# Gate and decay masks of a gated delta rule: GpSimd products replaced by ScalarE row scalings and one more accumulating matmul

## The chip, the core and the metric

The kernel runs on one core of a Trainium2 chip. The core has a matrix engine (TensorE, PE in the profile; PEld are its weight loads), a vector engine (VectorE, DVE), an activation engine (ScalarE, ACT), a general engine (GpSimd, POOL), and a queue that issues the transfers (SyncE, SP). Each engine works through its own list of instructions in order; between engines, an instruction waits until a semaphore says that its inputs are there. Matmuls write to PSUM banks of 128 x 512 float32 values; everything else lies in SBUF, as tiles of 128 partitions.

The metric is the time of one launch in device microseconds. A profile is one such launch, recorded by the hardware.

## What is computed

One decoder layer for 1024 prompt tokens (with zero state) and 8 x 8 sample tokens (each of the 8 sequences with a state of its own). One input projection feeds three groups: a convolution module, eight heads of a gated delta rule, and cross-attention into 256 memory tokens. Their outputs, gated, go through one output projection, and a layer norm follows. Cut to the delta rule, which the change touches:

```python
gcum = jnp.cumsum(g, axis=-1)                      # log decay, per head and token
incl = pos[:, None] >= pos[None, :]
decay = jnp.exp(jnp.where(incl, gcum[..., :, None] - gcum[..., None, :], -jnp.inf))
kb = k * beta[..., None]
m = jnp.where(strict, jnp.einsum("bnhik,bnhjk->bnhij", kb, k) * decay, 0.0)
tinv = lax.linalg.triangular_solve(eye + m, ...)
a_qk = jnp.einsum("bnhik,bnhjk->bnhij", q, k) * decay
def step(s, xs):                                   # chunk after chunk
    u = u0_c - jnp.einsum("bhck,bhkv->bhcv", w_c, s)
    o = jnp.einsum("bhck,bhkv->bhcv", qd_c, s) + jnp.einsum("bhij,bhjv->bhiv", aqk_c, u)
    s = s * gl_c + jnp.einsum("bhck,bhcv->bhkv", kd_c, u)
    return s, o
```

So each chunk needs a square matrix `decay`, the exponential of the difference of two running sums of `g`, zero where the second token comes later than the first. All inputs and outputs are float32.

## The kernel before

**Passes.** The input projection runs twice over its weights: first over the first 512 prompt tokens with the 64 sample tokens (576 columns, in two banks of 288), then over the last 512 prompt tokens (one bank of 512). A pass has 52 column tiles of 128 outputs, ordered by `ct_order`: for each head k, q, v and its gate, then the convolution's columns, then those of the memory. The first pass has the memory's own projection before column tile 44. Then comes the output projection in two groups of token tiles.

**Precision.** Float32 inputs are split in two parts of type fp32r, a high one (ACT copies it: `wh`, `xh`) and a low one (the rest, `wl`, `xl`, made by DVE, or by POOL for every other quarter up to the 450th). A product takes three fp32r matmuls (`mm3`). Weights arrive as 128 x 1024 pieces (`raw`) and are split in quarters of 512 columns (`split_quarter`). `gemm` calls `ensure(2)` ahead of a quarter's matmuls, so that two further quarters have been issued to ACT, DVE and POOL by then. There are four buffers for `wh` and four for `wl`.

**Side work.** Everything else (convolutions, delta rule, attention) is written as Python generators in a list, `Side`. After every group of matmuls `tick` steps those that are ready. Whether one is ready is asked of a planner, `Model`, that keeps a clock for each engine and a cost for each kind of instruction: for ACT 100 + 0.83 ns per element and 93 ns for each scale or bias that is a tile, for POOL's product of two tensors 100 + 2 ns per element, for an fp32r matmul its columns by 2.4 GHz. So the order of instructions on every engine is fixed when the program is built, and costs in the planner decide it. The four PSUM banks for side work are handed out by `getps` and given back by `relps`, at the planner's later clock of ACT and DVE.

**The delta rule.** A unit is one head in one pass: 512 tokens as four chunks of 128, so 16 units in all. `gen_gates` gives, for each pass, `gh` and `gl`, the high and low part of g. For a unit `gen_k` does, in this order: the products `gmh` and `gml` of the upper triangle `triu` (ones where column is at or past row) with g, for four chunks (lines 590 and 591); transposes of k and their squares (`jk`); two matmuls with `trilr`, the strict lower triangle, which add up g between two tokens for all four chunks in one bank `psD` (608, 609); `D`, its exponential, by ACT (611); the norms of k and beta (`kz`, `kzn`, 614 to 617); a power for v's scale (618); four products k by k in `psKK`; then `Dm` = D times `triu` (626), which clears what lies below the diagonal, and `D` times `kzn`, minus beta over the squared norm of k (628), both on POOL; `Y`, the product of `psKK` and D, on DVE (631). Y goes through DRAM into a solve by rows on DVE (`xt`, `X`, 652 to 656) and small matmuls (`U`). `gen_q` multiplies q by k with `Dm` (723), `gen_v` scales v, and `gen_chain` steps through the four chunks.

`gen_s` does the same for the sample tokens of a head, once per head in the first pass. Two tiles `S0` hold the eight states. After the matmul that reads them (896) and the solve's result `ut` (909) POOL multiplies them by their decay `egs` (911); `ux` repeats `ut` four times, masked by `bm4` (918), and ACT squares the output (`sqs`, 920).

`bc` repeats a matrix along a middle axis without a copy, `bl` repeats a column of values along the last axis.

Of the kernel before, what the change touches and what calls it, by code (L numbers as in the profile page):

```python
# [8 lines left out]
F32 = mybir.dt.float32  # L9
F32R = mybir.dt.float32r  # L10
AF = mybir.ActivationFunctionType
ALU = mybir.AluOpType
# [4 lines left out]
P = 128  # L17
# [144 lines left out]
def hybrid_step(ctx, tc, I, O):  # L162
    nc = tc.nc
    md = Model()
    act, dve, pool, pe, sp = (
        Proxy(md, n, e)
        for n, e in (("ACT", nc.scalar), ("DVE", nc.vector), ("POOL", nc.gpsimd), ("PE", nc.tensor), ("SP", nc.sync))
    )
# [8 lines left out]
    cst = sctx.enter_context(tc.tile_pool(name="cst", bufs=1))  # L177
# [6 lines left out]
    def nm(s):  # L184
        uid[0] += 1
        return f"{s}{uid[0]}"

    def W(shape, dt=F32, name="w"):
        return wk.tile(shape, dt, tag="W", bufs=NW, name=nm(name))

    def T5(shape, dt=F32, name="t"):
        return wk.tile(shape, dt, tag="T5", bufs=N5, name=nm(name))

    def Z(shape, name="z"):
        return wk.tile(shape, F32, tag="Z", bufs=NZ, name=nm(name))
# [4 lines left out]
    def getps(name="ps"):  # L200
        while live[0] >= 4 or min(freed) > md.clk["PE"]:
            yield "B"
        freed.remove(min(freed))
        live[0] += 1
        return pss.tile([P, 512], F32, tag="s", name=nm(name))
# [9 lines left out]
    def relps(n=1):  # L215
        live[0] -= n
        freed.extend([max(md.clk["ACT"], md.clk["DVE"]) + 100] * n)
# [79 lines left out]
    Y = {}  # L297
# [50 lines left out]
    ident = cst.tile([P, P], F32, name="ident")  # L348
    ones = cst.tile([P, P], F32, name="ones")
    triu = cst.tile([P, P], F32, name="triu")  # L350
    tril = cst.tile([P, P], F32, name="tril")
    trilr = cst.tile([P, P], F32R, name="trilr")
    bl8r = cst.tile([P, P], F32R, name="bl8r")
    bu8 = cst.tile([P, P], F32, name="bu8")
    auq = cst.tile([P, P], F32, name="auq")
    LV = (1, 2, 4)
# [3 lines left out]
    bm4 = cst.tile([P, 4], F32, name="bm4")  # L360
# [12 lines left out]
    def sel(out, in_, base, pattern, cm, fill=0.0):  # L373
        pool.affine_select(out=out, in_=in_, compare_op=ALU.is_ge, fill=fill, base=base, pattern=pattern,
                           channel_multiplier=cm)
# [2 lines left out]
    sel(tril, ones, -1, [[-1, P]], 1)  # L378
    sel(ident, triu, 0, [[-1, P]], 1)
    pool.tensor_copy(out=trilr, in_=tril)  # L380


    def bat(x):
# [51 lines left out]
    def bc(m, n=4):  # L435
        return m.unsqueeze(1).to_broadcast([m.shape[0], n, m.shape[1]])

    def bl(z, n, w):
        return z.unsqueeze(2).to_broadcast([z.shape[0], n, w])
# [86 lines left out]
    def transposes(ps, src, n=4, rows=P, cols=P):  # L526
        for c in range(n):
            pe.transpose(out=ps[0:cols, c * rows:(c + 1) * rows], in_=src[:, c * cols:(c + 1) * cols],
                         identity=ident[0:rows, 0:rows])

    def g3(ps, n=4, w=P):
        return ps[:, 0:n * w].rearrange("p (c n) -> p c n", c=n)

# [48 lines left out]
    def gen_k(u):  # L582
        p, h = u["p"], u["h"]
        while gates[p] is None or "ok_k" not in u:
            yield "B"
        gt = gates[p]
        u["gt"] = gt
        gmh = W([P, 4, P], F32R, name="gmh")
        gml = W([P, 4, P], F32R, name="gml")
        pool.tensor_tensor(out=gmh, in0=bc(triu), in1=bl(gt["gh"][:, 0:4, h].bitcast(F32), 4, P), op=ALU.mult)  # L590
        pool.tensor_tensor(out=gml, in0=bc(triu), in1=bl(gt["gl"][:, 0:4, h], 4, P), op=ALU.mult)
        kT = u["kT"]
        yield (kT,)
        psK = yield from getps()
# [3 lines left out]
        zn = Z([P, 4], name="kzn")  # L598
        kd = W([P, 4, P], name="kd")
        for c in range(4):  # L600
            jk = T5([P, P], name="jk")
            act.activation(out=jk, in_=psK[:, c * P:(c + 1) * P], func=AF.Square, accum_out=ss[:, c:c + 1])
        dve.tensor_tensor(out=kd, in0=g3(psK), in1=bl(gt["ed"][:, 0:4, h], 4, P), op=ALU.mult)
        relps()
        u["kd"] = kd
        yield (gmh, gml)
        psD = yield from getps()
        pe.matmul(out=psD, lhsT=trilr, rhs=gmh.rearrange("p a b -> p (a b)"), start=True, stop=False)
        pe.matmul(out=psD, lhsT=trilr, rhs=gml.rearrange("p a b -> p (a b)"), start=False, stop=True)
        D = W([P, 4, P], name="D")  # L610
        act.activation(out=D, in_=g3(psD), func=AF.Exp)
        relps()
        yield (z,)
# [7 lines left out]
        psKK = yield from getps()  # L621
        for c in range(4):
            pe.matmul(out=psKK[:, c * P:(c + 1) * P], lhsT=kT[:, c * P:(c + 1) * P], rhs=kT[:, c * P:(c + 1) * P],
                      start=True, stop=True)
        Dm = W([P, 4, P], name="Dm")
        pool.tensor_tensor(out=Dm, in0=D, in1=bc(triu), op=ALU.mult)
        u["Dm"] = Dm
        pool.tensor_tensor(out=D, in0=D, in1=bl(zn, 4, P), op=ALU.mult)
        yield (D,)
        Y = W([P, 4, P], name="Y")  # L630
        dve.tensor_tensor(out=Y, in0=g3(psKK), in1=D, op=ALU.mult)
        relps()
        n = nunit[0]
        nunit[0] += 1
# [41 lines left out]
        for c in range(4):  # L676
            for q in range(2):
                e, o = 64 * q, 64 * q + 32
                pe.matmul(out=ps[o:o + 32, 32 * c:32 * c + 32], lhsT=Y[e:e + 32, c, o:o + 32], rhs=Rc[e:e + 32, c],
                          start=True, stop=True)  # L680
# [6 lines left out]
        for c in range(4):  # L687
            for q in range(2):
                e, o = 64 * q, 64 * q + 32
                pe.matmul(out=ps[e:e + 32, 32 * c:32 * c + 32], lhsT=Pc[o:o + 32, c], rhs=Uc[o:o + 32, c], start=True,  # L690
                          stop=True)
# [13 lines left out]
        for c in range(4):  # L705
            pe.matmul(out=ps[0:64, 256 + 64 * c:320 + 64 * c], lhsT=P6[64:128, c], rhs=U[64:128, c, 64:128],
                      start=True, stop=True)
# [117 lines left out]
    def gen_s(u):  # L825
        h = u["h"]
        while not ("ok_k" in u and "ok_q" in u and "ok_v" in u) or gates[0] is None:
            yield "B"
        gt = gates[0]
        kq, vx = u["kq"], u["vx"]  # L830
        S0 = []
        for i in range(2):
# [3 lines left out]
        gmh, gml = (T5([P, P], F32R, name=n) for n in ("gmsh", "gmsl"))  # L836
        pool.tensor_scalar(out=gmh, in0=bu8, scalar1=gt["gh"][:, 4, h:h + 1].bitcast(F32), scalar2=0.0, op0=ALU.mult,
                           op1=ALU.add)
# [24 lines left out]
        D = T5([P, P], name="Ds")  # L863
        act.activation(out=D, in_=ps[:, 0:128], func=AF.Exp)
        Y, A = T5([P, P], name="Ys"), T5([P, P], name="As")
# [29 lines left out]
        for g in range(4):  # L895
            pe.matmul(out=ps[32 * g:32 * g + 32, 0:256], lhsT=kq[:, 32 * g:32 * g + 32],
                      rhs=S0[g // 2][:, 2 * (g % 2):2 * (g % 2) + 2, :].rearrange("p b v -> p (b v)"), start=True,
                      stop=True)
        r = T5([P, P], name="rs")
        dve.scalar_tensor_tensor(out=r, in0=ps[:, 0:128], scalar=gt["cs"][:, 0, h:h + 1], in1=vs, op0=ALU.mult,  # L900
                                 op1=ALU.add)
        dve.scalar_tensor_tensor(out=r, in0=ps[:, 128:256], scalar=gt["cs"][:, 1, h:h + 1], in1=r, op0=ALU.mult,
                                 op1=ALU.add)
# [4 lines left out]
        ut = T5([P, P], name="uts")  # L908
        dve.tensor_scalar(out=ut, in0=ps[:, 0:128], scalar1=B, scalar2=None, op0=ALU.mult)
        for i in range(2):  # L910
            pool.tensor_tensor(out=S0[i], in0=S0[i], in1=bl(gt["egs"][:, h, 4 * i:4 * i + 4], 4, P), op=ALU.mult)
        yield (ut,)
        pe.matmul(out=ps[:, 128:256], lhsT=A, rhs=ut, start=True, stop=True)
        o = T5([P, P], name="os")
        dve.tensor_tensor(out=o, in0=r, in1=ps[:, 128:256], op=ALU.add)
        relps()
        ux = W([P, 4, P], name="ux")
        pool.tensor_tensor(out=ux, in0=bc(ut), in1=bl(bm4, 4, P), op=ALU.mult)
        sq2 = T5([P, P], name="sqs")
        act.activation(out=sq2, in_=o, func=AF.Square, accum_out=z[:, 5:6])  # L920
        dve.scalar_tensor_tensor(out=z[:, 5:6], in0=z[:, 5:6], scalar=1.0 / P, in1=cq, op0=ALU.mult, op1=ALU.add)
# [4 lines left out]
        for v in range(0, 4, 2):  # L926
            for i in range(2):
                rows = slice(64 * i, 64 * i + 64)
                pe.matmul(out=psl[i][:, 128 * v:128 * v + 256], lhsT=kd[rows],
                          rhs=ux[rows, v:v + 2, :].rearrange("p a b -> p (a b)"), start=True, stop=True)  # L930
# [244 lines left out]
    def finish(p, t, psl):  # L1175
# [9 lines left out]
        if COL_Q <= c < COL_DGATE:  # L1185
# [13 lines left out]
            xr, xs = evac_qkv(p, ci, psl)  # L1199
            side.add(gen_conv4(p, ci, xr, xs, u, key))  # L1200
            side.add({"k": gen_k, "q": gen_q, "v": gen_v}[key](u))
            if key == "v":
                if p == 0:
                    side.add(gen_s(u))
                side.add(gen_chain(u))
# [468 lines left out]
```

## Time and profile before

| | us |
|---|---|
| median of three runs | 2069.68 |
| the three runs | 2062.01, 2069.68, 2070.32 |
| the profiled execution | 2062.28 |
| its span, first to last instruction | 2060.6 |

The mean clock that TensorE was granted is 0.990 of full speed.

The busy time of the engines in 40 equal slices of the span, each digit a tenth (9 is 90% or more), shows the stages: the first pass up to about slice 18, the second to about slice 31, then the output projection.

```profile
PE   8999999999999989999999999999989999999995
DVE  7777877887789984255787776779985433348447
ACT  5444444444433345364444444443326522235124
POOL 6434333343323242113333333322322100006003
```

A row of the grouped view names line, engine, operation, the tile written and the tiles read, the shapes, and the count; then the busy time of the group and the mean of one in ns; then how long the engine stood idle just before these instructions and what ended that. A row of the timeline has the start, the length (of several merged instructions together), and in brackets the idle time before. A row of the waits says who waited for whom: total, times, longest. Most instructions carry line 86, the planner's wrapper through which they are issued, so they are told apart by their tiles.

### The profile page before, as it was taken

How to read it: one execution, taken by the hardware profiler on the slowest of the kernel's cores; microseconds unless marked ns; L12 is line 12 of the kernel's file. 1: busy time of each engine (PE TensorE's matmuls, PEld its weight loads, DVE VectorE, ACT ScalarE, POOL GpSimd, SP SyncE). 2: the span in 40 equal slices, each digit the busy share in tenths (PEclk: the TensorE clock that was granted, in tenths of full speed). 3: DMA queues.
4: the chain of work that ended last, by engine and by line, in shares of the span. 5: the costliest groups of instructions: out<-in, count | busy, mean ns of one | idle time of the engine just before them, and what ended most of it. 6: DMA issues, size and time to landing. Idle time of an engine off the chain costs nothing. (4 is left out here: it accounts for less than half of the span.)

```text
span 2060.6 us, 33195 instructions
## 1 busy us (share of the span) xinstructions
PE 1973.7 (96%) x12156; PEld 1708.8 (83%) x12156; DVE 1429.6 (69%) x3190; ACT 844.7 (41%) x2013; POOL 605.7 (29%) x680
## 2 busy tenths in 40 slices
PE   8999999999999989999999999999989999999995
PEld 7999999999999969977777887787767788877784
DVE  7777877887789984255787776779985433348447
ACT  5444444444433345364444444443326522235124
POOL 6434333343323242113333333322322100006003
PEclk9999999999999999999999999999999999999998
DMA  5333233323233355354332223332232563345444
GB/s 205 93 100 93 88 96 102 102 82 99 86 99 97 104 165 167 109 176 149 96 93 89 76 89 104 102 93 82 90 102 92 156 205 105 106 159 182 141 132 144
DMA packets 107267, 239.50 MB, mean 116 GB/s; under 512 B 32224, under 2 KB 36576, under 8 KB 106848
## 3 DMA queue, kind: packets, MB, share of 16 engines
q1 hardware_dynamic: 107104, 237.39, 36.5%
q8 instruction: 95, 1.56, 0.3%
q14 instruction: 68, 0.56, 0.1%
HBM read 210.24 MB, written 27.10 MB: 115 GB/s over the span
## 5 line engine op out<-in xcount | busy, mean ns | idle before, releaser
L86 PE MATMUL m<-xh,wh 128*128 128x288 f32 (+1 forms) x2496 | 860.4, 345 | 7.4 <-ACT wh L86 7.4
L86 PE MATMUL m<-xh,wl 128*128 128x288 f32 (+1 forms) x2496 | 820.1, 329 | 12.7 <-DVE wl L86 9.6
L86 PE MATMUL m<-xl,wh 128*128 128x288 f32 (+1 forms) x2496 | 816.9, 327 | 0.0
L86 ACT CAST wh<-raw 128x512 fp32r<-128x512 f32 x592 | 359.5, 619 | 396.4 <-PE om L86 220.7
L86 POOL TENSOR_TENSOR wl<-raw,wh 128x512 fp32r<-128x512 f32 x221 | 308.5, 1396 | 725.5 <-ACT wh L86 695.5
L86 PEld LDWEIGHTS m<-xh,wh 128*128 128x128 f32 x2496 | 471.0, 189 | 54.3 <-issue 14.1
L86 PEld LDWEIGHTS m<-xh,wl 128*128 128x128 f32 x2496 | 469.7, 188 | 54.3 <-DVE wl L86 14.8
L86 PEld LDWEIGHTS m<-xl,wh 128*128 128x128 f32 x2496 | 471.4, 189 | 29.9 <-issue 2.4
L86 DVE TENSOR_TENSOR wl<-raw,wh 128x512 fp32r<-128x512 f32 x371 | 283.8, 771 | 265.9 <-ACT wh L86 265.5
L86 DVE SCALAR_TENSOR_TENSOR hc<-u,cvc,hc 128x512 f32<-128x512 f32 x360 | 241.5, 713 | 3.1
L86 PE MATMUL om<-wl,xh 128*128 128x512 f32 x576 | 226.8, 394 | 11.6 <-DVE wl L86 10.5
L86 PE MATMUL om<-wh,xh 128*128 128x512 f32 x576 | 226.9, 394 | 4.2 <-ACT wh L86 2.9
L86 PE MATMUL om<-wh,xl 128*128 128x512 f32 x512 | 200.7, 392 | 0.0
L86 DVE TENSOR_TENSOR xt<-mb,X 128x8 f32<-128x8 f32 (+30 forms) x496 | 182.3, 368 | 12.0 <-DVE mb L650 0.3
L86 DVE SCALAR_TENSOR_TENSOR cv<-xr,qcw,cv 128x512 f32<-128x512 f32 (+1 forms) x216 | 167.1, 774 | 7.7
L86 POOL TENSOR_TENSOR y<-y,lnb 128x512 f32<-128x512 f32 (+1 forms) x32 | 51.7, 1639 | 341.7 <-DVE y L86 222.6
L86 PEld LDWEIGHTS om<-wl,xh 128*128 128x128 f32 x576 | 108.9, 189 | 38.8 <-DVE wl L86 14.9
L86 ACT ACT_TABLE_LOAD x89 | 114.2, 1283 | 46.7 <-DVE smz L86 25.8
L86 PEld LDWEIGHTS om<-wh,xh 128*128 128x128 f32 x576 | 109.1, 189 | 29.1 <-ACT wh L86 4.6
L86 DVE TENSOR_REDUCE X<-xt 128x4 f32<-128x8 f32 (+30 forms) x496 | 110.1, 222 | 10.6
L86 PEld LDWEIGHTS om<-wh,xl 128*128 128x128 f32 x512 | 97.1, 190 | 20.2
L86 ACT ACTIVATE oi<-ps,GT 128x128 f32<-128x128 f32 x56 | 20.6, 367 | 207.8 <-DVE r L86 192.7
(309 smaller groups left out, 2010.1 us busy)
## 6 DMA issues: line engine op xcount, KB each, us to landing
raw<-in_wt_dram SPq DMA_DIRECT2D x208, 512.0 KB, 3.8
raw<-in_wo_dram SPq DMA_DIRECT2D x72, 512.0 KB, 3.8
mb<-ysc SPq DMA_DIRECT2D x128, 64.0 KB, 2.2
raw<-mx SPq DMA_DIRECT2D x16, 512.0 KB, 3.8
xt<-in_xp_dram SPq DMA_DIRECT2D x32, 256.0 KB, 4.4
out_y_p_dram<-y SPq DMA_DIRECT2D x32, 256.0 KB, 2.6
xraw<-in_xa_dram SPq DMA_DIRECT2D x16, 288.0 KB, 5.4
S<-in_sdelta_dram SPq DMA_DIRECT2D x16, 256.0 KB, 4.6
```

What stands on the lines that cost most here:

```text
L86: r = fn(**kw)
```

## The change

It takes four products of POOL out of `gen_k` and two out of `gen_s`:

- `gmh` and `gml` are each made by four ACT instructions, one for each chunk: `triu` times the chunk's column of g, as an activation Identity with a scale per partition (`rscale`).
- The matrix D is cleared below the diagonal ahead of the exponential: a third matmul adds -30000 there, with the identity as weights (`identr`) and the matrix `negr` repeated four times. The exponential of that is 0, so D itself serves as `Dm`, and POOL's product with `triu` is gone.
- D times `kzn` becomes four ACT scalings into a tile of its own, `Dz`, which Y reads. The tile Dm is no longer allocated, so the number of tiles is the same; D is now held until `gen_q` has read it.
- In `gen_s` each S0 tile is scaled by four ACT instructions, and `ux` is made by four.
- Two constants, `identr` and `negr`, are made by POOL at the start.

The planner charges ACT and PE for the new instructions as for others of their kind, so its clocks change, and the order of side work can.

```diff
+    identr = cst.tile([P, P], F32R, name="identr")
+    negr = cst.tile([P, P], F32R, name="negr")
...
+    pool.tensor_copy(out=identr, in_=ident)
+    pool.tensor_scalar(out=negr, in0=tril, scalar1=-30000.0, scalar2=0.0, op0=ALU.mult, op1=ALU.add)
...
+    def rscale(out, srcs, scales):
+        for c, (x, s) in enumerate(zip(srcs, scales)):
+            act.activation(out=out[:, c, :], in_=x, func=AF.Identity, scale=s)
...
-        pool.tensor_tensor(out=gmh, in0=bc(triu), in1=bl(gt["gh"][:, 0:4, h].bitcast(F32), 4, P), op=ALU.mult)
-        pool.tensor_tensor(out=gml, in0=bc(triu), in1=bl(gt["gl"][:, 0:4, h], 4, P), op=ALU.mult)
+        rscale(gmh, [triu] * 4, [gt["gh"][:, c, h:h + 1].bitcast(F32) for c in range(4)])
+        rscale(gml, [triu] * 4, [gt["gl"][:, c, h:h + 1] for c in range(4)])
...
-        pe.matmul(out=psD, lhsT=trilr, rhs=gml.rearrange("p a b -> p (a b)"), start=False, stop=True)
+        pe.matmul(out=psD, lhsT=trilr, rhs=gml.rearrange("p a b -> p (a b)"), start=False, stop=False)
+        pe.matmul(out=psD.rearrange("p (c n) -> p c n", c=4), lhsT=identr, rhs=bc(negr), start=False, stop=True)
...
-        Dm = W([P, 4, P], name="Dm")
-        pool.tensor_tensor(out=Dm, in0=D, in1=bc(triu), op=ALU.mult)
-        u["Dm"] = Dm
-        pool.tensor_tensor(out=D, in0=D, in1=bl(zn, 4, P), op=ALU.mult)
-        yield (D,)
+        u["Dm"] = D
+        Dz = W([P, 4, P], name="Dz")
+        rscale(Dz, [D[:, c, :] for c in range(4)], [zn[:, c:c + 1] for c in range(4)])
+        yield (Dz,)
         Y = W([P, 4, P], name="Y")
-        dve.tensor_tensor(out=Y, in0=g3(psKK), in1=D, op=ALU.mult)
+        dve.tensor_tensor(out=Y, in0=g3(psKK), in1=Dz, op=ALU.mult)
...
-            pool.tensor_tensor(out=S0[i], in0=S0[i], in1=bl(gt["egs"][:, h, 4 * i:4 * i + 4], 4, P), op=ALU.mult)
+            rscale(S0[i], [S0[i][:, b, :] for b in range(4)], [gt["egs"][:, h, 4 * i + b:4 * i + b + 1] for b in range(4)])
...
-        pool.tensor_tensor(out=ux, in0=bc(ut), in1=bl(bm4, 4, P), op=ALU.mult)
+        rscale(ux, [ut] * 4, [bm4[:, r:r + 1] for r in range(4)])
```

## The prediction, made before the changed kernel was run

> **What bounds the kernel now.** I read the page's totals first, then the busy time by stretch, then the waits of TensorE (PE).
>
> ```profile
> span 2060.6 us, 33195 instructions
> PE 1973.7 (96%) x12156; PEld 1708.8 (83%) x12156; DVE 1429.6 (69%) x3190; ACT 844.7 (41%) x2013; POOL 605.7 (29%) x680
> ...
> 200.00:400.00 200.00, 197.89 (x1639) 191.27 (x1637) 156.32 (x459) 88.60 (x263) 75.47 (x105) 1.00 0.31 95
> ...
> 1100.00:1300.00 200.00, 193.45 (x1100) 158.00 (x1099) 150.52 (x389) 90.35 (x257) 73.86 (x79) 1.00 0.30 92
> 1650.00:1850.00 200.00, 200.00 (x874) 164.17 (x873) 72.77 (x112) 48.17 (x81) 1.42 (x5) 0.99 0.44 143
> ```
>
> The columns of the stretches are busy time of PE, weight loads, DVE, ACT, POOL, then the granted clock. PE is idle for 87 us of 2060.6, and in 200 to 400 us for 2.1 of 200. A matmul's span overlaps the next, so I check the spacing: ten main matmuls start within 1.33 us in the first pass, so 0.133 us each, and 482 of width 512 take 111.62 us, 0.232 us each.
>
> ```profile
> 201.62 0.29 PE L86 MATMUL m<-xl,wh 128*128 128x288 f32 x1
> ...
> 202.95 0.29 PE L86 MATMUL m<-xh,wl 128*128 128x288 f32 x1
> ...
> 1910.20 111.62 PE om L86 x482
> ```
>
> So the end is set by the sum of PE's matmuls, and another engine counts only where PE waits for it:
>
> ```profile
> PE mm L86 <- DVE wl L86: 10.6, 3, 4.6
> PE om L86 <- DVE wl L86: 10.5, 6, 6.8
> PE m L86 <- DVE wl L86: 9.6, 12, 1.7
> PE m L86 <- ACT wh L86: 7.4, 1, 7.4
> PE ps L86 <- DVE rbuf L86: 5.3, 9, 1.2
> PE ps L86 <- DVE S L86: 3.6, 4, 2.0
> PE m L86 <- POOL wl L86: 3.0, 4, 1.1
> PE ps L86 <- DVE ut L86: 2.4, 5, 0.5
> ```
>
> No row names a mask (gmh, gml, D, S0, ux). The mm row is the memory projection, the om row the output projection, both away from the delta rule. What DVE's or POOL's lateness costs beside the delta rule is at most m, rbuf, S, POOL wl and ut: 9.6 + 5.3 + 3.6 + 3.0 + 2.4 = 23.9 us. This is the pool from which a gain can come.
>
> **Part by part. POOL loses six groups:**
>
> ```profile
> L86 POOL TENSOR_TENSOR Dm<-D,triu 128x512 f32<-128x512 f32 x16 | 21.7, 1355 | 0.0
> L86 POOL TENSOR_TENSOR gml<-triu,gl 128x512 fp32r<-128x512 f32 x16 | 19.7, 1228 | 0.0
> L86 POOL TENSOR_TENSOR D<-D,kzn 128x512 f32<-128x512 f32 x16 | 19.4, 1213 | 1.3
> L86 POOL TENSOR_TENSOR gmh<-triu,gh 128x512 fp32r<-128x512 f32 x16 | 19.2, 1197 | 0.0
> L86 POOL TENSOR_TENSOR S<-S,egs 128x512 f32<-128x512 f32 x16 | 16.8, 1069 | 28.8 <-PE ps L86 28.8
> L86 POOL TENSOR_TENSOR ux<-uts,bm 128x512 f32<-128x512 f32 x8 | 8.5, 1063 | 2.0 <-DVE uts L86 2.0
> ```
>
> 21.7 + 19.7 + 19.4 + 19.2 + 16.8 + 8.5 = 105.3 us, so POOL goes to about 500. POOL stands on no path that sets the end (only its 3.0 us of wl above), so directly this is worth 0 to 3 us.
>
> **ACT gains row scalings.** The same form stands in the trace, SBUF to SBUF with a scale per partition:
>
> ```profile
> 171.06 1.28 ACT L86 ACTIVATE ot<-ot,oz 128x128 f32<-128x128 f32 x4 [5.88 <-POOL oz L86]
> 172.25 0.29 ACT L86 ACTIVATE osT<-ps,dnw 128x64 f32<-128x64 f32 x1
> 172.44 0.62 ACT L86 ACTIVATE cv<-cv 128x512 f32<-128x512 f32 x1
> ```
>
> Four take 1.28 us, and a Silu (cv) follows without a table load, so Identity asks for none. Each of 16 units gets three sets of four (gmh, gml, Dz), each of the 8 sample heads three more (two S0, one ux): 16 x 3 + 8 x 3 = 72 sets, 72 x 1.28 = 92.2 us. ACT rises from 844.7 to 937 us, 45% of the span. In 200 to 400 us three heads bring 3 x 6 x 1.28 = 23 us: 88.6 becomes 112 of 200.
>
> [...]
>
> What covers the 92.2 us is ACT's own idle time. In the unit near 385 us (timelines of DVE, POOL and ACT):
>
> ```profile
> 388.69 0.17 DVE L86 TENSOR_SCALAR kzn<-kz 128x4 f32<-128x4 f32 x1
> 389.31 1.29 POOL L86 TENSOR_TENSOR Dm<-D,triu 128x512 f32<-128x512 f32 x1
> 390.67 1.37 POOL L86 TENSOR_TENSOR D<-D,kzn 128x512 f32<-128x512 f32 x1
> ...
> 387.43 0.60 ACT L86 CAST wh<-raw 128x512 fp32r<-128x512 f32 x1
> 391.52 0.28 ACT L86 ACTIVATE jk<-ps 128x128 f32<-128x128 f32 x1 [3.48 <-PE ps L86]
> ```
>
> Dz would run at 388.9 to 390.2, where ACT stood idle until 391.5, and Y could start some 1.8 us before POOL's D ended (392.0). Behind a scaling on ACT wait the casts wh, which feed PE. They are issued two weight quarters ahead: a quarter is 24 matmuls x 0.133 = 3.2 us in the first pass, so the lead is 6.4 us, and the longest burst, gmh with gml, is 2 x 1.28 = 2.56 us. The S0 scalings inherit POOL's wait for PE (28.8 us above); ACT waits at nearly that place already, for the sample output (rival 2 has the row). I cost ACT at 0. Without that cover the 92.2 us would bound the loss.
>
> **PE gains one matmul per unit**, identr against negr, 512 wide in fp32r. Its neighbours in the group and the dearest 512 row:
>
> ```profile
> L86 PE MATMUL ps<-gmh,trilr 128*128 128x512 f32 x16 | 6.8, 425 | 0.0
> L86 PE MATMUL ps<-PT,mvs 128*128 128x512 f32 x32 | 15.0, 592 | 0.0
> ```
>
> At the spacing 0.232 us it is 16 x 0.232 = 3.7 us. No matmul here reads a repeated block as this one does (negr four times); the bounds are 0, if it falls where PE waits anyhow, and 16 x 0.592 = 9.5 us. I take 3.7, since shape and type are those of gmh. It lies on PE's queue, so it counts in full.
>
> **DVE gets time back.** Its two-input work is longer while POOL works. The rows of wl on DVE in 1660 to 1840 us (POOL busy 1.42 us around there), then in 200 to 400 us (POOL 75.47), and cv in the latter:
>
> ```profile
> L86 DVE TENSOR_TENSOR wl<-raw,wh 128x512 fp32r<-128x512 f32 x56 | 38.3, 689 | 91.6 <-ACT wh L86 91.6
> ...
> L86 DVE TENSOR_TENSOR wl<-raw,wh 128x512 fp32r<-128x512 f32 x24 | 19.7, 821 | 8.2 <-ACT wh L86 8.2
> L86 DVE SCALAR_TENSOR_TENSOR cv<-xr,qcw,cv 128x512 f32<-128x512 f32 x27 | 23.0, 853 | 1.0
> ```
>
> 689 becomes 821. DVE can win between 0 and the 105.3 us that POOL no longer holds; I take 40. But PE waits for DVE in few places, and of the m row most lies in 1300 to 1560 us, where the last unit's masks end (D of the last unit is multiplied at 1341.4):
>
> ```profile
> PE m L86 <- DVE wl L86: 6.5, 9, 1.4
> ...
> L86 POOL TENSOR_TENSOR D<-D,kzn x16: 1039/1238/1372, 58.3 to 1341.4; 128x512 f32<-128x512 f32 x16
> ```
>
> So of the 23.9 us I give back 2 (bounds 0 and 23.9).
>
> Two 128 x 128 constants on POOL at the start lie ahead of the first unit and are each shorter than a 1.36 us product (bounds 0 and 2.7 us); PE's matmuls there don't read them, so I count 0. Table loads and the order of the side work may shift, since the planner's clocks of ACT and POOL change; I count 0 and give it a rival.
>
> **Sum**: +3.7 - 2.0 = +1.7 us. The profiled execution took 2062.28 us, so 2064.0. It is one of the low runs: the three timed ones are 2062.01, 2069.68 and 2070.32, their median 7.4 us above it. A median of such runs of the changed kernel lies between 2064.0 and 2071.4; I take **2068**.
>
> **Rivals.** (1) *DVE's relief reaches PE.* For it: wl on DVE takes 821 ns beside a busy POOL and 689 without, DVE is 75 to 78% busy in the delta-rule stretches, and wl, rbuf, S and ut on it end waits of PE. If all 23.9 us go, 2062.3 + 3.7 - 23.9 = 2042; if half, 2054. Against it: in 200 to 400 us PE has but 2.1 us to give. Faster by over 0.5% needs over 14 of the 23.9. Chance 0.12. [...]
>
> (2) *ACT becomes late with wh*: slower. ACT works in order; Dz now waits on ACT for kzn, which DVE makes late.
>
> ```profile
> 379.75 0.60 ACT L86 ACTIVATE D<-ps 128x512 f32<-128x512 f32 x1
> ...
> ACT sqs L86 <- DVE os L86: 29.7, 8, 7.1
> ```
>
> From D's end at 380.4 to kzn's at 388.9 are 8.5 us. If Dz stood in the queue right behind D, the next cast would leave 8.5 + 1.28 = 9.8 us later, 3.4 beyond the lead of 6.4: 16 x 3.4 = 54 us, 2120; in half of the units 27 us, 2093. It decides where ACT is held over 5.1 us ahead of Dz. Against it: casts stand between the two now (387.43), and ACT idles behind them. Chance 0.10.
>
> (3) *The planner's new order* moves side work and table loads about, some waits going and others coming.
>
> ```profile
> L86 ACT ACT_TABLE_LOAD x89 | 114.2, 1283 | 46.7 <-DVE smz L86 25.8
> ```
>
> A few loads of 1.28 us more or fewer end in ACT's idle time; for the waits I allow as much as the pool's m row, 10 us either way: 2054 to 2074 around 2064. It speaks for it that every cost in the planner's clock of POOL, ACT and PE near a unit changes, against it that PE is gapless in the first pass. Chance 0.18, nearly all within 0.5%.
>
> **Numbers.** Forecast 0.60. An effect under 0.5% (10 us) can't be told from none here. Faster 0.12, within 0.78 (0.60 + 0.18), slower 0.10. The range 2054 to 2080 takes in half of rival 1, rival 3, the runs' scatter, and the 9.5 us bound on the matmul over the upper 2071.4; it leaves out the further half of rival 1 and rival 2, some 0.15.
>
> **What would show it.** Right: 16 matmuls negr, identr at a spacing near 0.23 us; ACT near 937 us with no more than a few of 89 table loads more; POOL near 500; DVE down by 20 to 60 us, its wl in 200 to 400 us below 821 ns; PE idle in that stretch still about 2 us. Wrong: waits of PE for ACT wh in the delta-rule stretches (rival 2), or PE idle in 1100 to 1300 us falling from 6.5 us to near 0 (rival 1). The forecast fails if PE's idle time, not its sum of matmuls, moves by over 10 us.

## The result, and the profile after

The changed kernel took 2054.72 us, the median of five runs (2053.05 to 2056.60). The kernel before, run beside it five times, took 2065.51 us (2062.01 to 2070.32). The ratio is 0.9943, with a 95% interval of 0.9925 to 0.9962: **faster by 0.57%**, where the forecast was 2068 us and "within 0.5%". The time lies just inside the range of 2054 to 2080. A second measurement, five runs beside nine of the kernel before, gave 2054.75 against 2065.11 us, ratio 0.9946 [0.9934, 0.9959]. One of the five runs of kernel h below took 3928.41 us at a granted clock of 0.502; h's ratio is that of the other four, its median of all five (2049.95 without it).

The profiled execution of the changed kernel took 2054.72 us, that of the kernel before 2062.28. So the two traces differ by 7.6 us and the two medians by 10.8, because the profiled execution before was one of its low runs, as the prediction said. The totals of the page after:

```profile
span 2053.0 us, 33435 instructions
...
PE 1972.7 (96%) x12172; PEld 1712.2 (83%) x12172; DVE 1394.1 (68%) x3190; ACT 929.9 (45%) x2302; POOL 503.2 (25%) x594
```

Engine by engine the sums came out near the forecast: ACT 929.9 us (937 forecast), POOL 503.2 (about 500), DVE down by 1429.6 - 1394.1 = 35.5 (40). The new groups, line by line (the grouped view with shapes kept apart):

```profile
L86 ACT ACTIVATE gmh<-triu,gh 128x128 fp32r<-128x128 f32 x64 | 20.4, 392 | 0.0
L86 ACT ACTIVATE Dz<-D,kzn 128x128 f32<-128x128 f32 x64 | 20.5, 393 | 30.3 <-DVE kzn L86 25.5 <-issue 4.8
L86 PE MATMUL ps<-negr,identr 128*128 128x512 f32 x16 | 6.3, 392 | 0.0
```

Dz is the one new group in front of which ACT stands still for over 1 us: 25.5 us in all, waiting for kzn.

Where did the time go? Two marks divide the span: the first 512-wide main matmul `m` (start of the second pass) and the first `om` (start of the output projection). From the timeline of PE, before and then after:

```profile
908.36 0.50 PE L86 MATMUL m<-xh,wh 128*128 128x512 f32 x1
...
1637.72 0.50 PE L86 MATMUL om<-wh,xh 128*128 128x512 f32 x1
```

```profile
915.53 0.50 PE L86 MATMUL m<-xh,wh 128*128 128x512 f32 x1
...
1632.89 0.39 PE L86 MATMUL om<-wh,xh 128*128 128x512 f32 x1
```

The second pass took 729.4 us before and 717.4 after: **12.0 us won there**. The first pass took **7.2 us longer** (4.4 in the profile of the second measurement), and what follows the second pass 2.8 us less (0.7 there). A change that looks like half a per cent is thus a gain and a loss, each larger than the forecast's +1.7. The two profiles of the change differ by 2.8 us in the first pass, largely within the memory projection: in 700 to 800 us the granted clock was 0.91 in the first, 0.95 in the second and before.

The same is seen in the busy time by stretch (PE, weight loads, DVE, ACT, POOL, granted clock, DMA share, GB/s), first of before (its rows for the two short stretches stand in the prediction), then of after:

```profile
950.00:1640.00 690.00, 667.62 (x3511) 535.27 (x3510) 517.40 (x1146) 293.21 (x738) 214.84 (x211) 1.00 0.31 96
```

```profile
200.00:400.00 200.00, 197.07 (x1591) 189.92 (x1591) 147.57 (x456) 107.35 (x329) 49.48 (x84) 1.00 0.31 96
...
1100.00:1300.00 200.00, 199.86 (x1184) 164.31 (x1183) 150.17 (x407) 108.18 (x315) 52.33 (x62) 1.00 0.31 97
...
950.00:1640.00 690.00, 676.83 (x3581) 546.71 (x3581) 506.66 (x1159) 331.72 (x858) 183.18 (x185) 1.00 0.32 98
```

In 1100 to 1300 us PE's idle time fell from 6.55 us to 0.14. That is the marker that the prediction wrote down for rival 1. Over 950 to 1640 us it fell from 690 - 667.62 = 22.4 to 13.2 us. In the first pass, 200 to 400 us, it is 2.9 us where it was 2.1.

The waits of PE after the change (who waited for whom, total, times, longest):

```profile
PE m L86 <- DVE wl L86: 7.4, 10, 2.2
PE ps L86 <- DVE rbuf L86: 3.5, 6, 0.6
...
PE ps L86 <- ACT cv L86: 1.9, 6, 0.5
PE ps L86 <- DVE ut L86: 1.6, 1, 1.6
PE m L86 <- POOL wl L86: 1.5, 3, 0.7
...
PE ps L86 <- DVE S L86: 0.4, 2, 0.2
```

The pool of five rows that was 23.9 us is now 7.4 + 3.5 + 0.4 + 1.5 + 1.6 = 14.4: 9.5 us are gone (8.2 in the second measurement), where the forecast gave back 2. PE's idle time as a whole fell less, from 86.9 us to 80.3; its waits for ACT, for one, rose from 15.0 to 19.8 us (18.0). And DVE's rows, which the prediction had read as held up by POOL: wl in 200 to 400 us was 821 ns, now

```profile
L86 DVE TENSOR_TENSOR wl<-raw,wh 128x512 fp32r<-128x512 f32 x24 | 16.5, 686 | 16.1 <-ACT wh L86 16.1
```

and the convolution's cv in the second pass, 1000 to 1300 us, before and after:

```profile
L86 DVE SCALAR_TENSOR_TENSOR cv<-xr,qcw,cv 128x512 f32<-128x512 f32 x50 | 53.5, 1071 | 1.8
```

```profile
L86 DVE SCALAR_TENSOR_TENSOR cv<-xr,qcw,cv 128x512 f32<-128x512 f32 x48 | 43.8, 913 | 1.7
```

1071 ns became 913. Not every row shortened: the same form in 200 to 400 us took 853 ns before and 866 after.

A mean hides what happens here. The view of a tile gives the shortest, the median and the longest duration; of wl in 200 to 400 us, before and then after:

```profile
L86 DVE TENSOR_TENSOR wl<-raw,wh x24: 674/688/1771, 200.8 to 393.2; 128x512 fp32r<-128x512 f32 x24
```

```profile
L86 DVE TENSOR_TENSOR wl<-raw,wh x24: 681/684/693, 204.2 to 399.0; 128x512 fp32r<-128x512 f32 x24
```

The usual length did not change. Before, 21 of the 24 took 674 to 720 ns and three took 1754 to 1771, and each of these three began within 0.1 us behind a Dm product on POOL:

```profile
321.93 1.29 POOL L86 TENSOR_TENSOR Dm<-D,triu 128x512 f32<-128x512 f32 x1
322.00 1.77 DVE L86 TENSOR_TENSOR wl<-raw,wh 128x512 fp32r<-128x512 f32 x1
```

So 689 to 821 ns was not a general slowing: three instructions were longer by 1.1 us each, a little less than what was left of Dm's 1.29. It is the same with cv in 1000 to 1300 us: 31 of 50 took 750 to 754 ns before and 19 over 1400; after, 40 of 48 and eight. All eight run beside a wl on POOL, which the change leaves there.

### The profile page after: what moved, and what is told of

Same layout as the page of the kernel before. It is cut to its first block, busy times and chain, and to the rows that moved or that the text cites. A ratio compares the mean times of both kernels' runs of the same rounds, so it can differ in the third digit from the quotient of the medians.

```text
span 2053.0 us, 33435 instructions
## 1 busy us (share of the span) xinstructions
PE 1972.7 (96%) x12172; PEld 1712.2 (83%) x12172; DVE 1394.1 (68%) x3190; ACT 929.9 (45%) x2302; POOL 503.2 (25%) x594
## 4 chain that ended last, share of the span: by engine, by line
PE 43%; DVE 8%; issue 2%; ACT 1%; DMA 1%; POOL 1%; POOLq 0%; ACTq 0%; DVEq 0%
PE m L86 21%; PE om L86 17%; PE ps L86 5%; DVE hc L86 4%; DVE y L86 1%; DVE wl L86 1%; DMA raw<-mx 1%; ACT L86 0%; POOL y L86 0%; ACT wh L86 0%; POOL wl L86 0%; DMA raw<-in_wt_dram 0%; POOL lsum L86 0%; DMA out_y_p_dram<-y 0%; ACT hc L86 0%
## 5 line engine op out<-in xcount | busy, mean ns | idle before, releaser
L86 DVE TENSOR_TENSOR wl<-raw,wh 128x512 fp32r<-128x512 f32 x371 | 271.4, 737 | 281.7 <-ACT wh L86 279.5
L86 DVE TENSOR_TENSOR xt<-mb,X 128x8 f32<-128x8 f32 (+30 forms) x496 | 177.2, 357 | 11.7
L86 DVE SCALAR_TENSOR_TENSOR cv<-xr,qcw,cv 128x512 f32<-128x512 f32 (+1 forms) x216 | 155.6, 720 | 7.7
```

The source lines that it names most:

```text
L86: r = fn(**kw)
```

## The experiments

My theory after the result was that rival 1 had come true: POOL's products hold DVE, DVE's delay reaches PE, and taking the products away gives that back. Rival theories were that the planner's new order won the time, and that ACT's waits and the matmul explain the first pass's loss. The change bundles these: new instructions, and a new order of everything else that the planner derives from their costs. So most experiments either give the planner the *old* costs while issuing the new instructions ("old order": PE, DVE and SP then keep the order of before), or give it the *new* costs while issuing the old instructions ("new order"). The traces show the orders: in a, a2 and e the instructions of PE and of DVE come one by one as in the change, and in b, b2, b3 and b4 as in the kernel before, the added matmul and the scratch products apart. All times are medians; each ratio is to the kernel before on the same chip. The kernels were timed in four groups, in which the kernel before took 2064.01 us (a, b, d, e), 2065.11 (second measurement, a2, b2, h), 2064.64 (b3, b4, e2, f) and 2065.33 (h again, k). A difference across groups is therefore given twice where it matters: of the medians, and of the gains on the kernel before. Each stage is read from one profile, so that 1 to 3 us between two rows can be scatter (the change's own two rows are 2.8 us apart in the first pass). The table gives the stages from each profile (us): up to the second pass, the second pass, and the rest.

| kernel | median | ratio [95%] | first pass | second | rest |
|---|---|---|---|---|---|
| before | 2064.0 to 2065.5 | 1 | 908.4 | 729.4 | 422.9 |
| the change | 2054.72 | 0.9943 [0.9925, 0.9962] | 915.5 | 717.4 | 420.1 |
| the change, second measurement | 2054.75 | 0.9946 [0.9934, 0.9959] | 912.8 | 716.9 | 422.2 |
| a: new order, products on POOL, no Dm | 2061.57 | 0.9985 [0.9975, 0.9995] | 916.2 | 719.4 | 421.9 |
| a2: new order, old instructions | 2075.37 | 1.0052 [1.0039, 1.0066] | 918.2 | 725.3 | 423.0 |
| b: old order, all new instructions | 2089.65 | 1.0114 [1.0098, 1.0129] | 938.8 | 727.9 | 422.9 |
| b2: b, but Dz on POOL | 2057.62 | 0.9962 [0.9949, 0.9974] | 906.4 | 726.2 | 422.6 |
| b3: old order, only Dm replaced | 2061.73 | 0.9987 [0.9976, 0.9997] | 906.3 | 728.6 | 421.8 |
| b4: old order, only gm, S0, ux on ACT | 2057.23 | 0.9955 [0.9943, 0.9968] | 904.8 | 728.5 | 422.1 |
| d: the change + 64 matmuls | 2064.88 | 1.0000 [0.9988, 1.0011] | 917.1 | 723.0 | 423.0 |
| e: the change + POOL products | 2063.25 | 0.9995 [0.9986, 1.0005] | 919.6 | 721.1 | 422.7 |
| e2: the change + POOL memsets | 2053.92 | 0.9943 [0.9929, 0.9956] | 915.5 | 717.1 | 422.6 |
| f: the change in the first pass alone | 2067.71 | 1.0014 [1.0004, 1.0025] | 912.5 | 730.5 | 421.8 |
| h: in the second pass alone | 2050.39 | 0.9926 [0.9912, 0.9940] | 908.3 | 717.1 | 422.3 |
| h again | 2049.88 | 0.9920 [0.9902, 0.9937] | 908.7 | 717.8 | 422.1 |
| k: h, and b4 in the first pass | 2047.28 | 0.9912 [0.9899, 0.9926] | 906.2 | 715.7 | 422.3 |

The second measurement of the change, without any edit, stands as a measure for the others beside it:

> The changed kernel, on the same chip as the others of this group, to compare with: 2054.7 us if it is as in the first timing.

It gave 2054.75 us (2051.88 to 2055.57), the same as the first.

### Is it POOL's products? (e, e2, b4, a)

**e** gives POOL back its reading work, without any use: two products of constants into a scratch tile ahead of each set of scalings, the order of all else as in the change.

```diff
+    junk = cst.tile([P, 2, 112], F32, name="junk")
...
     def rscale(out, srcs, scales):
+        for _ in range(2):
+            nc.gpsimd.tensor_tensor(out=junk, in0=bc(triu[:, 0:112], 2), in1=bc(tril[:, 0:112], 2), op=ALU.mult)
         for c, (x, s) in enumerate(zip(srcs, scales)):
```

> The changed kernel, its order unchanged, with two POOL products of 128 x 224 into a scratch tile beside each set of four scalings (144 of them, some 85 to 105 us of POOL); nothing reads them. This brings back POOL's hold on DVE and its own queue, and not the products' place in the side chain. If DVE's relief is the gain: 2062 to 2068 us, with wl on DVE back above 800 ns in 200 to 400 us. If the shorter side chain or the order is the gain: within 2 us of 2055.

Measured: 2063.25 us, 8.5 above the change (9.6 by the gains). The group of scratch products on POOL, and the page's totals:

```profile
L538 POOL TENSOR_TENSOR junk<-triu,tril 128x224 f32<-128x224 f32 x144 | 106.4, 739 | 7.7
```

```profile
PE 1972.5 (96%) x12172; PEld 1711.2 (83%) x12172; DVE 1409.2 (68%) x3190; ACT 929.7 (45%) x2302; POOL 607.0 (29%) x738
```

POOL is back at 607 us, DVE is longer by 15.1 us though it has the same 3190 instructions, and PE has the same work but ends later: 4.1 us in the first pass, 3.7 in the second. The sign that was expected beside the time did not come: wl in 200 to 400 us took 690 ns, not over 800, and DVE got back only 15.1 of the 35.5 us. The scratch products do not stand where Dm stood, just ahead of wl, and at 739 ns they are shorter; so the total is near that of before, but other DVE instructions meet them.

**e2** keeps POOL's queue just as full, with memsets, which write but read nothing:

```diff
     def rscale(out, srcs, scales):
+        for _ in range(5):
+            nc.gpsimd.memset(junk, 0.0)
         for c, (x, s) in enumerate(zip(srcs, scales)):
```

> As e_pool_dummy, but POOL is kept busy by writes alone (five memsets of 128 x 224 beside each set of scalings, about as long as the two products). If the dummies' 8.5 us came from POOL's reads holding up DVE, this stays at 2054 to 2057 us with wl on DVE below 720 ns in 200 to 400 us; if from POOL's own queue being late with wl and the powers, 2062 to 2065 us.

```profile
L538 POOL MEMSET junk<- 128x224 f32 x360 | 103.7, 288 | 18.1
```

Measured: 2053.92 us, 0.8 below the change, with DVE at 1394.1 us as in the change. So 103.7 us of memsets on POOL cost nothing by themselves; 106.4 us of products that read SBUF cost 8.5 us. The memsets are also shorter (288 ns against 739), but the traces tell the two apart one by one: of DVE's wl and cv of 512 columns that ran beside memsets and nothing else of POOL, 24 in e2, all took 678 to 754 ns; of those that ran beside scratch products alone, 18 in e, twelve took 1039 to 1149. In these two runs it was not POOL's queue that counted but what its reading products did to DVE: its busy time rose by 15.1 us in e and by 0.0 us in e2. Why products that read lengthen DVE's instructions and memsets do not, no run shows.

**b4** does the converse without any new order: in the old order, gmh, gml, S0 and ux go to ACT, while both products with D stay on POOL and there is no added matmul.

```diff
+    def rscale(out, srcs, scales, ins):
+        md.run("POOL", 100 + 2.0 * _free(out), [out], ins)
+        for c, (x, s) in enumerate(zip(srcs, scales)):
+            nc.scalar.activation(out=out[:, c, :], in_=x, func=AF.Identity, scale=s)
...
-        pool.tensor_tensor(out=gmh, in0=bc(triu), in1=bl(gt["gh"][:, 0:4, h].bitcast(F32), 4, P), op=ALU.mult)
+        rscale(gmh, [triu] * 4, [gt["gh"][:, c, h:h + 1].bitcast(F32) for c in range(4)], [triu, gt["gh"]])
```

(`gml`, `S0` and `ux` likewise; `md.run` charges the planner as before.)

> The kernel before in its own order, with the other part: gmh, gml, S0 and ux on ACT (64.2 us less on POOL), Dm and D by kzn stay POOL products, no added matmul. If POOL's load is what gains, 2055 to 2060 us; if only the way to Y counts, 2065 us as before.

Measured: 2057.23 us, 7.4 below the kernel before (2064.64 there). Here neither the order nor PE's work changed, so this is the relief by itself, for 64.2 of the 105.3 us of products, less whatever the scalings cost on ACT.

**a** has the order of the change and its matmul in place of the Dm product, but the other products are on POOL again:

```diff
         for c, (x, s) in enumerate(zip(srcs, scales)):
-            act.activation(out=out[:, c, :], in_=x, func=AF.Identity, scale=s)
+            md.run("ACT", 100 + 0.83 * _free(x) + 93, [out], [x, s])
+        nc.gpsimd.tensor_tensor(out=out, in0=in0, in1=in1, op=ALU.mult)
```

> The order of the changed kernel to the instruction on PE, DVE and SP, with the added matmul, but gmh, gml, Dz, S0 and ux made by POOL products again (Dm's product stays away, its work is the added matmul's). Theory X: the gain is gone, 2066 to 2070 us. Theory O: 2055 us, with DVE as long as before (about 1425 us).

Measured: 2061.57 us, between the two expectations and 6.8 above the change (7.9 by the gains), with POOL at 578.7 us and DVE at 1422.9. Three measurements of the relief, some 7 to 10 us, lie close together though they differ in order and in the products concerned.

### Is it the order? (a2, b, b2, b3)

**a2** issues the old instructions in the order of the change: as `a`, with the Dm product kept on POOL and no matmul (the planner is charged for one).

```diff
+        nc.gpsimd.tensor_tensor(out=D, in0=D, in1=bc(triu), op=ALU.mult)
         u["Dm"] = D
         Dz = W([P, 4, P], name="Dz")
         rscale(Dz, [D[:, c, :] for c in range(4)], [zn[:, c:c + 1] for c in range(4)], D, bl(zn, 4, P))
```

> The instructions of the kernel before (all six POOL products, no added matmul) in the changed kernel's order on PE, DVE and SP. With the order alone (theory O) it gains on the kernel before: a_new_order_pool's 2061.6 less some 2.5 us of the matmul, plus the Dm product, so 2058 to 2061. If order does nothing by itself (theory X): 2064, as before.

Measured: 2075.37 us (2068.59 to 2077.42), **10.3 above** the kernel before, which neither theory had expected. The new order by itself wins nothing. Its profile, taken of the lowest run, puts 9.8 us of loss into the first pass and 4.0 of gain into the second:

```profile
918.22 0.50 PE L86 MATMUL m<-xh,wh 128*128 128x512 f32 x1
...
1643.55 0.39 PE L86 MATMUL om<-wh,xh 128*128 128x512 f32 x1
```

That run is 6.8 us below the median of a2; where the others lose more, no profile tells. And a2 differs from a in one thing only, the Dm product in place of the added matmul, yet a gains 2.4 us on the kernel before where a2 loses 10.3. So in the new order this one step is worth 12.7 us; in the old order it is worth 2.9 (b3 below).

**b** is the converse: all of the change's instructions, in the old order (b4's edits, the matmul, and Dz by ACT in the same manner).

```diff
+        nc.tensor.matmul(out=psD.rearrange("p (c n) -> p c n", c=4), lhsT=identr, rhs=bc(negr), start=False, stop=True)
...
-        Dm = W([P, 4, P], name="Dm")
-        pool.tensor_tensor(out=Dm, in0=D, in1=bc(triu), op=ALU.mult)
...
+        md.run("POOL", 100 + 2.0 * _free(D), [D], [D])
+        u["Dm"] = D
+        Dz = W([P, 4, P], name="Dz")
+        rscale(Dz, [D[:, c, :] for c in range(4)], [zn[:, c:c + 1] for c in range(4)], [zn])
```

> All of the change's instructions (ACT scalings, the added matmul, no POOL products), but issued in the order of the kernel before: the planner is charged as if the POOL products were still there, so that PE, DVE and SP have the order of before to the instruction, and the added matmul apart. If the gain comes from the execution (theory X: POOL no longer holds DVE and the side chain is shorter), this takes about 2055 us, as the changed kernel. If it comes from the planner's new order (theory O), it takes the time of before plus the 3.7 us of the added matmul, 2066 to 2070 us.

Measured: 2089.65 us, **25.6 above** the kernel before, outside both expectations. Its waits of PE, then ACT and PE around one of them:

```profile
PE ps L86 <- ACT cv L86: 19.8, 7, 3.3
```

```profile
257.68 1.28 ACT L538 ACTIVATE Dz<-D,kzn 128x128 f32<-128x128 f32 x4 [6.68 <-DVE kzn L86]
258.86 0.60 ACT L86 CAST wh<-raw 128x512 fp32r<-128x512 f32 x1
259.48 1.28 ACT L86 ACT_TABLE_LOAD   x1
260.78 0.63 ACT L86 ACTIVATE cv<-cv 128x512 f32<-128x512 f32 x1
...
261.46 1.96 PE L86 MATMUL ps<-cv,cv 128*128 128x128 f32 x8 [3.26 <-ACT cv L86]
```

Read it from the bottom: PE stands still for 3.26 us before the product of q and k, because the Silu that makes q's cv ended late; that Silu stood behind a table load and a cast, which stood behind Dz; and Dz held ACT for 6.68 us until DVE had made kzn. The table shows the loss in the first pass (30.4 us over eight heads, 3.8 each); the second has none. Not all of it is waiting: six waits for cv there make 19.4 us, and PE's busy time in that pass rose by 11.5 us, of which the eight added matmuls explain at most 1.9; the granted clock in 100 to 600 us was 0.98 where it had been 1.00. That is rival 2's mechanism, with another victim: q's Silu, not the casts wh.

**b2** moves Dz alone back to POOL:

```diff
-        rscale(Dz, [D[:, c, :] for c in range(4)], [zn[:, c:c + 1] for c in range(4)], [zn])
+        md.run("POOL", 100 + 2.0 * _free(Dz), [Dz], [zn])
+        nc.gpsimd.tensor_tensor(out=Dz, in0=D, in1=bl(zn, 4, P), op=ALU.mult)
```

> As b_old_order_act (all on ACT, the order of before), but Dz alone is made by POOL. If b's 25 us come from ACT held at Dz until kzn is there, so that the Silu of q and PE's product behind it are late (3.2 us of PE idle in each of six heads), these waits go: 2064 to 2068 us. If they come from ACT's added work as such, it stays above 2080 us.

Measured: 2057.62 us, 7.5 below the kernel before where b was 25.6 above; the expectation had been 2064 to 2068. One group of instructions on another engine is worth 33.1 us in this order: Dz on ACT was more than the whole loss of b.

**b3** is the matmul in place of the Dm product and nothing else, in the old order.

```diff
+        nc.tensor.matmul(out=psD.rearrange("p (c n) -> p c n", c=4), lhsT=identr, rhs=bc(negr), start=False, stop=True)
...
-        pool.tensor_tensor(out=Dm, in0=D, in1=bc(triu), op=ALU.mult)
...
+        u["Dm"] = D
...
+        nc.gpsimd.tensor_tensor(out=Dz, in0=D, in1=bl(zn, 4, P), op=ALU.mult)
```

> The kernel before in its own order, with one part of the change: Dm's product is replaced by the added matmul; gmh, gml, Dz, S0 and ux stay on POOL. If taking Dm's 1.36 us out of the way to Y (POOL: a power, Dm, then D by kzn) is what gains, about 2058 us, as b2_old_order_dz_pool. If POOL's load (here only 21.7 of 105.3 us less) is what gains, 2063 to 2067 us.

Measured: 2061.73 us, 2.9 below the kernel before, just outside of no change. PE's added matmul is paid for by POOL's product. b3 and b4 do not add up: 2.9 + 7.4 = 10.3, but b2, which holds the edits of both, gains 7.5. That is left open.

### What does the matmul cost? (d)

```diff
+        nc.tensor.matmul(out=psD.rearrange("p (c n) -> p c n", c=4), lhsT=identr, rhs=bc(negr), start=False, stop=False)
         pe.matmul(out=psD.rearrange("p (c n) -> p c n", c=4), lhsT=identr, rhs=bc(negr), start=False, stop=True)
```

(four such lines; the mask is then five times as negative, and its exponential is 0 all the same)

> The changed kernel, its order unchanged, with the added matmul of negr five times per unit instead of once (the sum stays so negative that the exponential is 0): 64 matmuls of width 512 more. By the prediction's price, 0.232 us each and in full on PE's path: 14.8 us more, 2069.5 us. If PE has slack that hides it, less than 5 us more.

Measured: 2064.88 us, 10.1 above the change's 2054.75 for 64 matmuls, 0.158 us each (11.2 and 0.175 by the gains). The sixteen of the change cost some 2.5 to 2.8 us. PE's busy time rose by 14.3 us, 0.223 each, and its idle time fell by 4.2: a part of them falls where PE would have waited.

### Which pass? (f, h, k)

**f** and **h** make the change in the first or the second pass alone, and the planner plans anew; the sample tokens' part goes with the first. The edit is of this kind at each place (here h against the change):

```diff
-        rscale(gmh, [triu] * 4, [gt["gh"][:, c, h:h + 1].bitcast(F32) for c in range(4)])
...
+        if p == 1:
+            rscale(gmh, [triu] * 4, [gt["gh"][:, c, h:h + 1].bitcast(F32) for c in range(4)])
...
+        else:
+            pool.tensor_tensor(out=gmh, in0=bc(triu), in1=bl(gt["gh"][:, 0:4, h].bitcast(F32), 4, P), op=ALU.mult)
```

> The change in the first pass alone (gen_s included), the second as before, planned anew. By the profiles' split, the first pass loses 5 to 7 us and the rest gains nothing: 2069 to 2072 us. If the passes can't be taken apart, 2055 to 2060 us.

> The change in the second pass alone: the first pass (p = 0) has the POOL products of before, in gen_k and gen_s, and no added matmul; planned anew. If the profiles' split holds (first pass 7 us longer, second pass and the rest 15 us shorter), 2048 to 2051 us. If the second pass gains only because of what the first one leaves behind, 2055 us or more.

Measured: f 2067.71 us, 3.1 above the kernel before, less than the 2069 to 2072 expected; h 2050.39 us, 14.7 below it. Together -11.6 us, against -10.4 for the whole change beside h: the passes add up, and the first-pass half is a loss.

After these the first pass was still open: is it the scalings on ACT that cost it time, or the new order? **k** puts b4's edits into the first pass, in the old order, and leaves the second as in h (`rscale0` is the `rscale` of b4; the lines are against h):

```diff
         if p == 1:
             rscale(gmh, [triu] * 4, [gt["gh"][:, c, h:h + 1].bitcast(F32) for c in range(4)])
         else:
-            pool.tensor_tensor(out=gmh, in0=bc(triu), in1=bl(gt["gh"][:, 0:4, h].bitcast(F32), 4, P), op=ALU.mult)
+            rscale0(gmh, [triu] * 4, [gt["gh"][:, c, h:h + 1].bitcast(F32) for c in range(4)], [triu, gt["gh"]])
```

> The second pass is as in h_second_pass; in the first pass gmh, gml, S0 and ux go to ACT, Dm and D times kzn stay on POOL, and the planner is charged as before, so that PE, DVE and SP keep their order of h_second_pass there. If the first pass of the changed kernel loses because of the planner's new order, and the scalings on ACT are no cost, the first pass must gain here what it gained in b4_old_order_gm_s (3.6 us by the start of the second pass), and the time is 3 to 7 us below h_second_pass: 2044 to 2047. If the scalings themselves cost the first pass something (f_first_pass was 3.1 us slower), the time is at or above that of h_second_pass: 2050 to 2054.

> The change in the second pass alone, once more beside the former: 2050.4 within 2 us if the first measurement stands; if it was luck of that chip, nearer to the 2054.7 of the changed kernel.

Measured: h again 2049.88 us, k **2047.28 us** (2046.05 to 2048.06), ratio 0.9912 [0.9899, 0.9926]. k is 2.6 below h beside it, a little less than the 3 to 7 expected, and its first pass gains 2.2 us where the change lost 7.2. So the scalings of gmh, gml, S0 and ux are no cost there (Dz and the matmul are not in k's first pass); that the order is one, a2 shows. It is also the fastest version: it beats the kernel before by 18.0 us and the change by 7.4. Its page:

```profile
span 2044.3 us, 33409 instructions
...
PE 1967.3 (96%) x12164; PEld 1709.3 (84%) x12164; DVE 1399.7 (68%) x3190; ACT 919.4 (45%) x2270; POOL 523.0 (26%) x610
```

## Why the prediction was wrong, step by step

- **What bounds the kernel**: right. PE is 95 to 96% busy in every kernel of the table, and POOL's queue as such was worth nothing in e2 (103.7 us of memsets, 2053.92 us against the change's 2054.72).
- **ACT +92.2 us, costed at 0**: nearly right. ACT's busy time rose by 85.2 us and table loads went from 89 to 90. PE's waits for ACT rose by 4.8 us (3.0 in the second measurement); the longest new one, for wh, 2.9 us, lies in the second pass's first 20 us.
- **PE +3.7 us**: too much by some 1. The cost at the margin is 0.158 to 0.175 us a matmul (d), not the spacing of 0.232.
- **DVE -40 us**: right, 35.5, and wl in 200 to 400 us fell to 686 ns, below the 821 as forecast. But 821 was read as DVE's general pace beside a busy POOL; it was the mean of 21 instructions of the usual length and three that took 1.1 us more, each behind a Dm product.
- **"So of the 23.9 us I give back 2"**: this is the step that failed, by its size. The waits of that pool fell by 9.5 us, and the relief measured by itself is some 7 to 10 us (b4, a, e). Two reasons had been given for the 2. One was that PE has but 2.1 us to give in 200 to 400 us. That is a first-pass stretch; in 950 to 1640 us PE had 22.4 us of idle time. The other was that most of the m row lies where the last masks end. But the S row (3.6 to 0.4 us), rbuf (5.3 to 3.5) and POOL's wl (3.0 to 1.5) gave more together than the m row (9.6 to 7.4), and they were in the pool, unargued.
- **The sum**: 2062.28 + 2.5 - 9.5 = 2055.3 with the two measured terms, against 2054.72 for the profiled execution. That it fits so well is partly luck, since the order's effects, of both signs, are in it too. The general sign of failure, PE's idle time moving by over 10 us, did not come: it moved by 6.6, because gain and loss cancel in it.
- **Rival 1** (0.12) is what happened, and near its middle case (2054). Its marker, PE's idle time in 1100 to 1300 us falling from 6.5 us to near 0, came true to the letter, but it does not mark DVE's relief alone. That idle time is 4.2 us in b2 and 5.2 in b4 (relief, old order), 6.8 in a2 and 3.1 in a (new order), and with POOL's reads put back in e only 1.7. It takes the order and the new instructions together.
- **Rival 2** (0.10) did not happen, but b shows that its mechanism is there: Dz held for kzn, and what stands behind it late. The price per unit was close (3.4 us by the prediction, waits of up to 3.3 in b), the victim was another, q's Silu and not wh, and the second pass was spared. In the planner's new order ACT still waits for kzn, 25.5 us in place of 48.6, but PE's waits for cv are 1.9 us in place of 19.8.
- **Rival 3** (0.18, nearly all within 0.5%), the new order, counted at 0 in the sum: it moved as much as the bounds of 10 us allowed for. By itself it costs 10.3 us (a2). In that order, Dm's product replaced by the matmul then gains 12.7 us (a against a2) and the other products moved to ACT 7.9 (the change against a, by the gains). In the old order the Dm step gains only 2.9. The difference lies largely in the second pass, 725.3 us in a2 and 719.4 in a. That the Dm product stands on the way to Y at a worse place in the new order is likely, not shown. The first pass of the change can be accounted for in the profile of the second measurement, 4.4 us longer: PE's idle time there rose by 2.5 us (new waits for cv 1.9, ut 1.6, Pc 1.1, ux 0.5, less what wl, rbuf and S gave back) and its busy time by 1.9, eight matmuls of 0.232. Why a2, without these matmuls, loses 9.8 us there, half of it in busy time, is open.

## What to carry to other kernels

That POOL is off the path did not make its products free here (8.5 us in e): look at how long DVE's instructions are beside them and without them (the shortest and the longest, not the mean: here wl's 674 and 1771 ns), and at who waits for DVE in the stretch with the *most* idle time, not in the one with the least. An instruction moved to another engine took its waits along (here 6.7 us for kzn in b), and what stood behind it in that engine's list paid (q's Silu, and PE with 3.3 us), so the order should be planned with the move, and then measured by itself: here the new order cost 10.3 us. Where a change goes into two stages with different slack, measure each alone: here one half was worth 15 us, the other cost 3.

## What the runs showed of the hardware that was not expected

POOL's 360 memsets in e2 (103.7 us) left DVE's busy time at 1394.1 us and the kernel at 2053.92 us (2054.72 without them), while 144 products of about the same total time in e (106.4 us) cost DVE 15.1 us and the kernel 8.5. In 200 to 400 us before, DVE's two-input wl of 512 columns came in two separate lengths, not in a spread: 674 to 720 ns, or 1754 to 1771 behind a Dm product of 1.28 to 1.29 us. One DVE instruction with a single tensor input, a product with a column of scalars, also shortened: from 766 ns before to 479 after in 200 to 400 us.

```profile
L86 DVE TENSOR_SCALAR cv<-xr,qcw 128x512 f32<-128x512 f32 x9 | 6.9, 766 | 0.0
```

```profile
L86 DVE TENSOR_SCALAR cv<-xr,qcw 128x512 f32<-128x512 f32 x9 | 4.3, 479 | 0.0
```

In e, with POOL's reading work back, it was 478 ns in that stretch, and the 64-column form of the same instruction went the other way, from 482 ns before to 596 after. What decides it was not followed up.
